# The linear attention's off-diagonal blocks over the array's column groups, in one PSUM tile for both parts of the sequence

## The chip, the cores and the metric

The kernel runs on one core of a Trainium2 chip. The metric is the device time of one execution in microseconds (us). TensorE (PE) multiplies matrices: it holds one operand, the weights, in its 128 by 128 array, streams the other past it and writes the result to PSUM. VectorE (DVE) and ScalarE (ACT) work elementwise and can read PSUM; GpSimd (POOL) and SyncE (SP) mostly issue transfers here.

## The reference

The reference is a trunk of two layers for one sequence of 256 positions and a width of 2048, in float32. Layer 0 has dilated sliding-window softmax attention in parallel with gated linear attention, layer 1 an S5 state-space part in parallel with HGRN2, which is gated linear attention again. Each layer has one input projection, a SiLU gate and one output projection, with RMSNorm before it. Cut to the part that the change is about:

```python
def chunked_gated_linear_attention(q, k, v, log_g):
    '''S_t = diag(g_t) S_{t-1} + k_t^T v_t ; o_t = q_t S_t, evaluated chunkwise.'''
    ...
        diff = bi[:, :, None] - bi[:, None, :]
        decay = jnp.exp(jnp.where(causal, diff, -jnp.inf))
        scores = jnp.einsum('bihk,bjhk,bijhk->bhij', qi, ki, decay)
        intra = jnp.einsum('bhij,bjhv->bihv', scores, vi)
```

So the score of query i and key j is the sum over the head's 128 channels of q times k times the product of the gates between j and i. Layer 0 does it for 4 heads, layer 1 for 8.

## The kernel before

**Projections.** `gemm_fm` (L174, matmul at L181) and `gemm_tm` (L193, matmul at L200) run through the weights in groups of 4 by 128 rows and 512 columns. `load_split` (L143) loads a group of 1 MB through SP's queue, rounds it to a high part `wh` on ScalarE (L168) and takes the rest `wl` on VectorE (L169); both are marked urgent and have three buffers. Three products per block (high by high, high by low, low by high) then go to a PSUM tile of the pool `pg`.

**Linear attention.** `gla` (L276) takes gates f, queries q and keys k as tiles of 128 channels by 4 heads by 256 positions. It is called once in layer 0 (L402) and twice in layer 1 (L675, four heads each). The scores go to the tile `AT` (named gA), which holds for each head three blocks of 128 keys by 128 queries: the first 128 positions with themselves (index 0), the first 128 as keys with the last 128 as queries (index 1), and the last 128 with themselves (index 2). The loop at L294 doubles a length h from 1 to 128. At level h the sequence falls into runs of 2h positions, and the queries in the second half of each run meet the keys in its first half. Between levels, VectorE multiplies the second halves of the queries (`Qp`, named gQ; L324) and the first halves of the keys (L325) by the gates over the next run (`Tc`), so that each level's product has its decay already in it.

- Levels 1 to 16 (`LV`): `small_blocks` (L281, matmul at L287) multiplies every 32 positions with themselves, and a masked copy (L296) picks what belongs to the level. Its four blocks of 32 write to partitions 0, 32, 64 and 96 of one PSUM tile in turn.
- Levels 32 and 64, the lines that change: for each of the two parts t of 128 positions there is a PSUM tile of its own. Each run of 2h positions, starting at j0, has one matmul per head (L308) of h keys by h queries over 128 channels; it writes to partitions j0 to j0 + h, the place that the block has in `AT`. A copy on VectorE per run (L311) brings all four heads' blocks to `AT`.
- Level 128: one matmul per head (L316) and a copy on ScalarE.

L339 then multiplies the scores with v.

**Order and buffers.** All of these tiles come from the pool `pm` (L65), four buffers of 128 partitions by 512 float32, which the softmax attention, the S5 part (L583, L622, L627) and its preparation (L1027) use too. L1027 and L622 multiply 128 rows by 64 weight columns and write to partitions 0 to 63 and 64 to 127 in turn. The order of the instructions on each engine is not that of the program text: a planner that simulates the run works it out when the kernel is built (L1126), with the urgent ones ahead, and it places the waits. On the chip each engine takes its instructions in that order.

Of the kernel before, what the change touches and what calls it, by code (L numbers as in the profile page):

```python
# [57 lines left out]
def trunk(ctx: ExitStack, tc: tile.TileContext, I, out):  # L58
    nc = tc.nc
    V, G, A, T = nc.vector, nc.gpsimd, nc.scalar, nc.tensor  # L60
# [26 lines left out]
    def col(o, n=1):  # L87
        return vec[:, o:o + n]

    def pm_tile(name="pm"):  # L90
        return pm.tile([128, 512], F32, name=name, tag="pm")

    def rsqrt(y, a, n, tag):
        it = small.tile([128, n], I32, name=tag + "i")
        ah = small.tile([128, n], F32, name=tag + "h")
        u = small.tile([128, n], F32, name=tag + "u")
        V.tensor_scalar(it, a.bitcast(I32), 1, None, op0=OP.logical_shift_right)
        V.tensor_scalar(y.bitcast(I32), it, -1.0, float(0x5F3759DF), op0=OP.mult, op1=OP.add)
        V.tensor_scalar(ah, a, -0.5, None, op0=OP.mult)
        for _ in range(3):  # L100
            V.tensor_tensor(u, y, y, op=OP.mult)
            V.tensor_tensor(u, u, ah, op=OP.mult)
            V.scalar_tensor_tensor(y, u, 1.5, y, op0=OP.add, op1=OP.mult)
# [70 lines left out]
    def gemm_fm(src, groups, ah, al, mid=None, order=None):  # L174
        ps = pg.tile([128, 4, S], F32, name="pg")
        last = groups * 4 - 1
        for i, kt, wh, wl in _iter(src, groups, mid, order):
            for n, (w, a) in enumerate(((wh, ah), (wh, al), (wl, ah))):
                for c in range(4):
                    cs = slice(c * 128, (c + 1) * 128)  # L180
                    state["mm"] = T.matmul(ps[:, c], w[:, cs], a[:, kt],  # L181
                                           start=(i == 0 and n == 0 and c % 2 == 0),
                                           stop=(i == last and n == 2), skip_group_check=True)
        return ps
# [8 lines left out]
    def gemm_tm(src, groups, ah, al, mid=None, order=None):  # L193
        ps = pg.tile([128, 2, 512], F32, name="pg")
        last = groups * 4 - 1
        for i, kt, wh, wl in _iter(src, groups, mid, order):
            for n, (w, a) in enumerate(((wh, ah), (wh, al), (wl, ah))):
                for t in range(2):
                    ts_ = slice(t * 128, (t + 1) * 128)
                    state["mm"] = T.matmul(ps[:, t], a[:, kt, ts_], w, start=(i == 0 and n == 0),  # L200
                                           stop=(i == last and n == 2), skip_group_check=True)
        return ps
# [5 lines left out]
    def bc(ap, n):  # L208
        return ap[:, None, :].to_broadcast([128, n, ap.shape[1]])

    def gla_tiles():
        return (mix.tile([128, 4, S], F32, name="gf"), mix.tile([128, 4, S], F32, name="gq"),
                mix.tile([128, 4, S], F32, name="gk"))
# [26 lines left out]
    f, q, k = gla_tiles()  # L240
# [30 lines left out]
    AT = const.tile([128, 4, 3, 128], F32, name="gA")  # L271
# [4 lines left out]
    def gla(f, q, k, v, dv, o0, rc=None):  # L276
        Qp = mix.tile([128, 4, S], F32, name="gQ")
        Dg = mix.tile([128, 2, 4, 32], F32, name="gD")
        V.tensor_mul(Qp, q, f)

        def small_blocks(Q):  # L281
            ps = pm_tile()[:, 0:256].rearrange("p (t h i) -> p t h i", t=2, h=4)
            for t in range(2):
                for hd in range(4):
                    for b in range(4):
                        r = slice(t * 128 + 32 * b, t * 128 + 32 * b + 32)
                        T.matmul(ps[32 * b:32 * b + 32, t, hd], k[:, hd, r], Q[:, hd, r], start=True, stop=True)  # L287
            return ps.rearrange("p t h i -> p (t h) i")

        Df = Dg.rearrange("p t h i -> p (t h) i")  # L290
        V.tensor_mul(Df, small_blocks(q), bc(cst[:, C_ID32:C_ID32 + 32], 8))
        Tc = f
        h = 1
        while True:  # L294
            if h in LV:
                V.copy_predicated(Df, bc(msk[:, LV.index(h)], 8), small_blocks(Qp))  # L296
                if h == LV[-1]:
                    for b in range(4):
                        r = slice(32 * b, 32 * b + 32)
                        for t in range(2):  # L300
                            A.activation(AT[r, :, 2 * t, r], Dg[r, t], AF.Copy)
            elif h < 128:
                for t in range(2):
                    ps = pm_tile().rearrange("p (h i) -> p h i", h=4)
                    for j0 in range(0, 128, 2 * h):
                        for hd in range(4):
                            b = t * 128 + j0
                            T.matmul(ps[j0:j0 + h, hd, j0 + h:j0 + 2 * h], k[:, hd, b:b + h],  # L308
                                     Qp[:, hd, b + h:b + 2 * h], start=True, stop=True)
                    for j0 in range(0, 128, 2 * h):  # L310
                        V.tensor_copy(AT[j0:j0 + h, :, 2 * t, j0 + h:j0 + 2 * h],  # L311
                                      ps[j0:j0 + h, :, j0 + h:j0 + 2 * h])
            else:
                ps = pm_tile()
                for hd in range(4):
                    T.matmul(ps[:, hd * 128:(hd + 1) * 128], k[:, hd, 0:128], Qp[:, hd, 128:256],  # L316
                             start=True, stop=True)
                A.activation(AT[:, :, 1], ps.rearrange("p (h i) -> p h i", h=4), AF.Copy)
                break
            nb = 4 * S // (2 * h)  # L320
            Qv = Qp.rearrange("p a s -> p (a s)").rearrange("p (n two h) -> p n two h", two=2, h=h)
            Kv = k.rearrange("p a s -> p (a s)").rearrange("p (n two h) -> p n two h", two=2, h=h)
            Tv = (Tc.rearrange("p a s -> p (a s)") if h == 1 else Tc).rearrange("p (n two) -> p n two", two=2)
            V.tensor_mul(Qv[:, :, 1], Qv[:, :, 1], Tv[:, :, 0:1].to_broadcast([128, nb, h]))  # L324
            V.tensor_mul(Kv[:, :, 0], Kv[:, :, 0], Tv[:, :, 1:2].to_broadcast([128, nb, h]))  # L325
            Tn = mix.tile([128, nb], F32, name=f"gT{h}")
            V.tensor_mul(Tn, Tv[:, :, 0], Tv[:, :, 1])
            Tc = Tn
            h *= 2
        o = [mix.tile([128, 4, dv], F32, name="go", tag=n) for n in ("gf", "gQ")]  # L330
        ssq = small.tile([128, 2, 4], F32, name="ssq")
        junk = mix.tile([128, 256], F32, name="junk", tag="gT1")
        hp = 512 // dv
        for t in range(2):
            for h0 in range(0, 4, hp):
                ps = pm_tile()
                for hd in range(h0, h0 + hp):
                    for j in range(t + 1):
                        T.matmul(ps[:, (hd - h0) * dv:(hd - h0 + 1) * dv], AT[:, hd, t + j],  # L339
                                 v[:, j, hd * dv:(hd + 1) * dv], start=(j == 0), stop=(j == t))  # L340
                A.activation(o[t][:, h0:h0 + hp], ps.rearrange("p (h d) -> p h d", d=dv), AF.Copy,
                             scale=1.0 if rc is None else rc[:, t:t + 1])
                for hd in range(h0, h0 + hp):
                    A.activation(junk[:, 0:dv], o[t][:, hd], AF.Square, accum_out=ssq[:, t, hd:hd + 1])
        ms = small.tile([128, 8], F32, name="hms")
        V.tensor_scalar(ms, ssq.rearrange("p a b -> p (a b)"), 1.0 / dv, EPS, op0=OP.mult, op1=OP.add)
        rs = small.tile([128, 8], F32, name="hrs")
        rsqrt(rs, ms, 8, "hr")
        for t in range(2):
            for hd in range(4):  # L350
                A.activation(og[:, t, o0 + hd * dv:o0 + hd * dv + dv], o[t][:, hd], AF.Copy,
                             scale=rs[:, t * 4 + hd:t * 4 + hd + 1])
# [23 lines left out]
    for h0 in range(0, 4, 2):  # L376
        ps = pm_tile().rearrange("p (n s) -> p n s", n=2)
        for n in range(2):
            T.matmul(ps[:, n], wgt[:, (h0 + n) * 128:(h0 + n + 1) * 128], glo, start=True, stop=True)
        for n in range(2):  # L380
            b = col(V_BG + h0 + n)
# [160 lines left out]
    for b in range(2):  # L542
        ps = gemm_fm(w1[b], 4, xh, xl)
# [119 lines left out]
    for half in range(2):  # L663
        f, q, k = gla_tiles()
# [24 lines left out]
    for b in range(2):  # L689
        ps = gemm_fm(I["wg"][b], 2, yh[:, 8:16], yl[:, 8:16])  # L690
# [54 lines left out]
    for b in range(3):  # L745
        res, h2 = residual(b)
        ps = gemm_tm(I["wo1"][b], 4, yh, yl, order=(2, 3, 0, 1))
# [4 lines left out]
    for half in range(2):  # L752
        ps = pg.tile([128, 2, 512], F32, name="pg")
# [385 lines left out]
```

## Time and profile before

| | |
|---|---|
| median of 3 runs | 888.54 us (887.33 to 891.26) |
| the profiled execution | 894.61 us, of which the span is 892.7 us |
| TensorE busy, granted clock | 874.1 us, 0.996 |
| VectorE, ScalarE busy | 636.0 us, 473.1 us |
| records at L308 | 144, the first at 131.7 us, the last at 710.9 us |
| moved from and to memory | 180.40 MB, a mean of 202 GB/s |

The span runs from the first instruction to the last. In the profile L308 is line 308, `pm<-gQ,gk` a group's output and inputs by the program's names, and PEld the loading of weights. Each float32 matmul of L287, L308, L622 and L1027 leaves two records, so that a count there is twice the number of matmuls. A record of TensorE lasts longer than its share of the stream, as matmuls overlap; what a group takes is read from the start of its first record to the start of the next group.

### The profile page before, as it was taken

The numbers are of one execution on the slowest core, as the hardware profiler recorded it, in microseconds if no ns is written. First come the engines' busy times: TensorE is split into PE (matmuls) and PEld (weight loads), VectorE is DVE, ScalarE is ACT, GpSimd is POOL, SyncE is SP. The second block draws the span as 40 slices with busy tenths as digits, with TensorE's granted clock in tenths as the row PEclk, the third lists the DMA queues.
The fourth block names the chain that finished last, engine by engine and source line by source line (L and its number), as shares of the span: only waits on it lengthen the run. The fifth ranks groups of instructions, "written<-read, shape, count | busy, mean of one in ns | idle before, by whom it ended". The sixth has DMA issues, their size and how long they took to land.

```text
span 892.7 us, 18688 instructions
## 1 busy us (share of the span) xinstructions
PE 874.1 (98%) x7728; PEld 804.5 (90%) x7728; DVE 636.0 (71%) x1197; ACT 473.1 (53%) x715; POOL 54.4 (6%) x106
## 2 busy tenths in 40 slices
PE   8999999999999999999999999999999999999995
PEld 8987899888998899999999999899867899988894
DVE  7987975888869868755575586877977655665562
ACT  7654546665655765644443345455545475444451
POOL 0001100111101101000000001100110000000000
PEclk9999999999999999999999999999999999999998
DMA  9827744777756655555575766754654455544432
GB/s 316 318 99 217 257 159 146 231 253 217 264 193 220 223 179 182 206 189 189 190 270 195 267 211 227 247 192 166 222 170 160 183 189 189 189 171 179 176 136 94
DMA packets 40388, 180.40 MB, mean 202 GB/s; under 512 B 12720, under 2 KB 14256, under 8 KB 22768
## 3 DMA queue, kind: packets, MB, share of 16 engines
q1 hardware_dynamic: 29440, 154.99, 49.5%
q0 software_dynamic: 7984, 22.69, 7.7%
q10 hardware_dynamic: 2880, 1.54, 0.6%
q8 instruction: 60, 0.98, 0.4%
q14 instruction: 24, 0.20, 0.1%
HBM read 166.48 MB, written 12.71 MB: 201 GB/s over the span
## 4 chain that ended last, share of the span: by engine, by line
PE 74%; DVE 8%; ACT 6%; DMA 5%; issue 5%; SPq 0%; POOL 0%; POOLq 0%; DVEq 0%; ACTq 0%
PE pg L181 48%; PE pg L200 17%; DVE wl L169 2%; PE pg L758 2%; DMA tabs<-pc 2%; ACT wh L168 1%; PE pm L287 1%; DMA E<-ed 1%; PE pm L339 1%; DMA s5y<-ys 1%; ACT bb L1021 1%; DMA raw<-in_w_dram 1%; ACT x L1039 1%; PE pm L308 1%; DVE PP L1005 1%
## 5 line engine op out<-in xcount | busy, mean ns | idle before, releaser
L168 ACT ACTIVATE wh<-raw 128x1024 fp32r<-128x1024 f32 (+2 forms) x276 | 287.6, 1046 | 325.0 <-PE pg L181 187.6
L169 DVE TENSOR_TENSOR wl<-raw,wh 128x1024 fp32r<-128x1024 f32 (+2 forms) x276 | 332.6, 1207 | 173.7 <-ACT wh L168 165.0
L181 PE MATMUL pg<-xh,wh 128*128 128x256 f32 x1024 | 162.8, 281 | 1.8 <-ACT wh L168 1.7
L181 PE MATMUL pg<-xl,wh 128*128 128x256 f32 x1024 | 163.8, 280 | 0.0
L181 PE MATMUL pg<-xh,wl 128*128 128x256 f32 x1024 | 163.4, 281 | 0.1
L181 PEld LDWEIGHTS pg<-xh,wh 128*128 128x128 f32 x1024 | 137.4, 188 | 3.7 <-ACT wh L168 3.1
L181 PEld LDWEIGHTS pg<-xl,wh 128*128 128x128 f32 x1024 | 138.0, 188 | 0.8 <-issue 0.3
L181 PEld LDWEIGHTS pg<-xh,wl 128*128 128x128 f32 x1024 | 137.9, 189 | 0.8 <-DVE wl L169 0.3
L200 PE MATMUL pg<-wh,xh 128*128 128x512 f32 x320 | 100.4, 395 | 1.8 <-ACT wh L168 1.8
L200 PE MATMUL pg<-wl,xh 128*128 128x512 f32 x320 | 101.0, 396 | 0.5 <-DVE wl L169 0.4
L200 PE MATMUL pg<-wh,xl 128*128 128x512 f32 x320 | 101.0, 395 | 0.0
L200 PEld LDWEIGHTS pg<-wh,xh 128*128 128x128 f32 x320 | 59.3, 188 | 14.8 <-ACT wh L168 2.2
L200 PEld LDWEIGHTS pg<-wl,xh 128*128 128x128 f32 x320 | 59.5, 188 | 14.1 <-DVE wl L169 1.3
L200 PEld LDWEIGHTS pg<-wh,xl 128*128 128x128 f32 x320 | 59.9, 188 | 12.8
L181 PE MATMUL pg<-yh,wh 128*128 128x256 f32 x320 | 50.8, 281 | 0.0
L181 PE MATMUL pg<-yl,wh 128*128 128x256 f32 x320 | 50.6, 281 | 0.0
L181 PE MATMUL pg<-yh,wl 128*128 128x256 f32 x320 | 50.6, 281 | 0.0
L181 PEld LDWEIGHTS pg<-yl,wh 128*128 128x128 f32 x320 | 43.4, 190 | 0.1
L181 PEld LDWEIGHTS pg<-yh,wh 128*128 128x128 f32 x320 | 43.2, 189 | 0.1
L181 PEld LDWEIGHTS pg<-yh,wl 128*128 128x128 f32 x320 | 43.1, 189 | 0.0
L967 POOL DMA_DIRECT2D tabs<-pc x44 | 23.8, 546 | 167.0 <-DVE x L977 43.7
L200 PE MATMUL pg<-wh,yh 128*128 128x512 f32 x96 | 30.1, 394 | 0.0
(350 smaller groups left out, 994.0 us busy)
## 6 DMA issues: line engine op xcount, KB each, us to landing
raw<-in_w_dram SPq DMA_DIRECT2D x100, 1024.0 KB, 5.0
raw<-in_wo_dram SPq DMA_DIRECT2D x28, 1024.0 KB, 4.8
tb<-tabs POOLq DMA_DIRECT2D x8, 768.0 KB, 6.4
tabs<-pc POOLq DMA_DIRECT2D x20, 256.0 KB, 5.7
raw<-in_wg_dram SPq DMA_DIRECT2D x4, 1024.0 KB, 4.8
raw<-in_wo1l_dram SPq DMA_DIRECT2D x4, 1024.0 KB, 4.8
raw<-in_w_dram SPq DMA_DIRECT2D x6, 512.0 KB, 7.4
tabs<-pc POOLq DMA_DIRECT2D x24, 128.0 KB, 4.9
```

Of the source, the lines that this page charges most:

```text
L168: state["wh"] = A.activation(w, r, AF.Copy)
L169: V.tensor_sub(l, r, w)
L181: state["mm"] = T.matmul(ps[:, c], w[:, cs], a[:, kt], start=(i == 0 and n == 0 and c % 2 == 0), stop=(i == last and n == 2), skip_group_c ...
L200: state["mm"] = T.matmul(ps[:, t], a[:, kt, ts_], w, start=(i == 0 and n == 0), stop=(i == last and n == 2), skip_group_check=True)
L287: T.matmul(ps[32 * b:32 * b + 32, t, hd], k[:, hd, r], Q[:, hd, r], start=True, stop=True)
L308: T.matmul(ps[j0:j0 + h, hd, j0 + h:j0 + 2 * h], k[:, hd, b:b + h], Qp[:, hd, b + h:b + 2 * h], start=True, stop=True)
L339: T.matmul(ps[:, (hd - h0) * dv:(hd - h0 + 1) * dv], AT[:, hd, t + j], v[:, j, hd * dv:(hd + 1) * dv], start=(j == 0), stop=(j == t))
L758: T.matmul(ps[:, t, 0:256], a_[:, kt, ts_], w_, start=(kt == 0 and n == 0), stop=(kt == KT - 1 and n == 2), skip_group_check=True)
L967: nc.gpsimd.dma_start(tabs[qt, dst, n], t[src].rearrange("p a b -> p (a b)"))
L1005: V.scalar_tensor_tensor(PP[half[1 - g], g].rearrange("p a b c -> p (a b c)"), x1[half[g]], -1.0, x2[half[g]], op0=OP.mult, op1=OP.subtract)
L1021: A.activation(bb[half[g ^ n], g], z[n][half[g]].unsqueeze(2).to_broadcast([64, 8, 4, 16]), AF.Copy)
L1039: A.activation(v8(x1)[:, r_], cst[:, C_ID64:C_ID64 + 64], AF.Copy, scale=vec[:, V_D + 8 * qt + r_:V_D + 8 * qt + r_ + 1])
```

## The change

At levels 32 and 64 both parts of the sequence now share one PSUM tile. Run n of the whole sequence (four at h = 32, two at h = 64) writes its four heads' blocks to partitions h n to h n + h, in the first 4h columns of the tile, and the inner loop goes over the runs, not over the heads. The copies bring each run's block from there to the same place in `AT` as before. The numbers of matmuls (16 and 8) and of copies (4 and 2) per call stay, and so do their sizes.

```diff
             elif h < 128:
-                for t in range(2):
-                    ps = pm_tile().rearrange("p (h i) -> p h i", h=4)
-                    for j0 in range(0, 128, 2 * h):
-                        for hd in range(4):
-                            b = t * 128 + j0
-                            T.matmul(ps[j0:j0 + h, hd, j0 + h:j0 + 2 * h], k[:, hd, b:b + h],
-                                     Qp[:, hd, b + h:b + 2 * h], start=True, stop=True)
-                    for j0 in range(0, 128, 2 * h):
-                        V.tensor_copy(AT[j0:j0 + h, :, 2 * t, j0 + h:j0 + 2 * h],
-                                      ps[j0:j0 + h, :, j0 + h:j0 + 2 * h])
+                ps = pm_tile()[:, 0:4 * h].rearrange("p (h i) -> p h i", h=4)
+                for hd in range(4):
+                    for n in range(128 // h):
+                        b = 2 * h * n
+                        T.matmul(ps[h * n:h * n + h, hd], k[:, hd, b:b + h], Qp[:, hd, b + h:b + 2 * h],
+                                 start=True, stop=True)
+                for n in range(128 // h):
+                    t, j0 = divmod(2 * h * n, 128)
+                    V.tensor_copy(AT[j0:j0 + h, :, 2 * t, j0 + h:j0 + 2 * h], ps[h * n:h * n + h])
             else:
```

## The prediction

> **What bounds the kernel now.** I read the page first, then who waited for whom, the timeline of TensorE around the bursts that the change rewrites, and the grouped lines of VectorE.
>
> ```profile
> span 892.7 us, 18688 instructions
> PE 874.1 (98%) x7728; PEld 804.5 (90%) x7728; DVE 636.0 (71%) x1197; ACT 473.1 (53%) x715; POOL 54.4 (6%) x106
> PEclk9999999999999999999999999999999999999998
> ```
>
> TensorE is busy for 98% of the span at full granted clock, VectorE for 71%. A busy row can hide waiting, so the waits of TensorE come next (columns: who waited for whom, total us, times, longest).
>
> ```profile
> PE pg L200 <- ACT wh L168: 1.8, 1, 1.8
> PE pg L181 <- ACT wh L168: 1.7, 3, 0.7
> PE pm L435 <- ACT pT L433: 1.2, 1, 1.2
> PE pm L287 <- DVE gk L325: 1.1, 1, 1.1
> ...
> PE pg L758 <- DVE h L721: 0.5, 1, 0.5
> PE pg L200 <- DVE wl L169: 0.4, 2, 0.2
> PE pm L431 <- DVE pr L428: 0.4, 1, 0.4
> ```
>
> These rows add up to 7.1 us in 892.7. So TensorE's own time sets the end, and time taken off its stream should reach the end unless one of these few waits swallows it. The linear attention stands inside that stream: its matmuls come as short bursts between the projections' matmuls.
>
> **The change part by part.** L308 issues, per call of gla, 16 matmuls at h = 32 and 8 at h = 64; the trace has two records for each (float32), so 32 and 16 records a burst. gla is called three times, which makes six bursts. The time that a burst takes from the stream is its start to the start of the next projection matmul:
>
> ```profile
> 131.73 0.90 PE L308 MATMUL pm<-gQ,gk 128*32 128x32 f32 x32
> 132.56 0.39 PE L181 MATMUL pg<-xl,wh 128*128 128x256 f32 x1
> ...
> 137.54 1.14 PE L308 MATMUL pm<-gQ,gk 128*64 128x64 f32 x16
> 138.62 0.62 PE L181 MATMUL pg<-xh,wh 128*128 128x256 f32 x3
> ```
>
> That is 0.83 us and 1.08 us. The other four bursts agree, the middle call's in the chain that ended last (start, us, what) and the last call's in the timeline:
>
> ```profile
> 601.88 0.83 PE pm L308 x32
> ...
> 607.12 1.07 PE pm L308 x16
> ```
>
> ```profile
> 702.79 0.90 PE L308 MATMUL pm<-gQ,gk 128*32 128x32 f32 x32
> 703.62 0.50 PE L200 MATMUL pg<-wh,xl 128*128 128x512 f32 x1
> ...
> 710.02 1.15 PE L308 MATMUL pm<-gQ,gk 128*64 128x64 f32 x16
> 711.10 0.50 PE L200 MATMUL pg<-wh,xh 128*128 128x512 f32 x1
> ```
>
> The number and shape of the matmuls stay; what changes is where each writes, and so which columns of the array hold its weights. Before, at h = 64 all eight write partitions 0 to 63; at h = 32 four in a row write 0 to 31, then four 64 to 95. Afterwards neighbours go to different places: 0, 32, 64, 96 in turn at h = 32, and 0, 64 in turn at h = 64. The trace has both patterns already. L622 alternates between partitions 0 and 64 with 64 weight columns and 64 moving ones, 16 records like h = 64; L1027 does the same 32 times; L287 goes round all four places with 32 by 32, 64 records or, in a fragment, 4.
>
> ```profile
> 534.21 0.69 PE L622 MATMUL pm<-X,tb 128*64 128x64 f32 x16
> 534.82 0.56 PE L627 MATMUL pm<-t,tb 64*64 64x63 f32 x12
> ...
> 335.27 1.15 PE L1027 MATMUL pm<-PP,bb 128*64 128x64 f32 x32
> 336.35 0.88 PE L504 MATMUL pm<-cst,gz 128*128 128x128 f32 x6
> ...
> 126.87 0.76 PE L287 MATMUL pm<-gQ,gk 128*32 128x32 f32 x64
> 127.56 0.61 PE L181 MATMUL pg<-xh,wl 128*128 128x256 f32 x3
> ...
> 103.54 0.26 PE L287 MATMUL pm<-gq,gk 128*32 128x32 f32 x4
> 103.73 0.73 PE L200 MATMUL pg<-wl,xh 128*128 128x512 f32 x2
> ```
>
> At h = 64 the new burst is L622's: 16 records in 0.61 us, where L308 takes 1.08: a gain of 0.47. At h = 32 it lies on L287's line: 64 records take 0.69 and 4 take 0.19, so one costs (0.69 - 0.19)/60 = 0.0083 us and the fixed part is 0.16; 32 records come to 0.16 + 32 x 0.0083 = 0.42, where L308 takes 0.83: a gain of 0.41. Together 0.88 us per call and **2.64 us** for three.
>
> A rule speaks against this. The Trainium skill, page "TensorE: Matmul & The Clock Gate", section "Part 3: Packing small matmuls — row/col tiling", says that a weight load overlaps running matmuls only when its row group differs; all these matmuls use all 128 rows, so by that rule the sum would be 0. The trace disagrees: at the same 128 rows and 64 columns L308 takes 1.08 us for 16 records, L1027 1.08 us for 32. Part 2 of that page, section "Back-to-back issue gap", gives small matmuls an issue floor of about 25 ns; by it 32 records would need an estimated 0.8 us and h = 32 would gain nothing. The trace disagrees there too: 64 records of L287 take 0.69 us.
>
> For the unknown size of the overlap I keep both ends: nothing gained, 0; and all fixed parts gone too, 2.64 + 6 x 0.16 = 3.6 us. I take 2.64, since L622 is the same shape in the same order.
>
> **VectorE.** The copies of L311 stay 18 in number and keep their shapes and destinations. Their source becomes contiguous and starts at partition h n. Rows of such copies, and the one that reads a whole contiguous PSUM row block:
>
> ```profile
> L169 DVE TENSOR_TENSOR wl<-raw,wh 128x1024 fp32r<-128x1024 f32 x270 | 329.5, 1222 | 172.1 <-ACT wh L168 163.5 <-ACT junk L344 3.6 <-PE pg L181 2.7
> ...
> L296 DVE COPY_PREDICATED gD<-msk,pm 128x256 f32<-128x256 int32 x15 | 6.7, 448 | 1.6 <-PE pm L287 1.3
> L311 DVE COPY gA<-pm 32x128 f32<-32x128 f32 x12 | 3.4, 283 | 0.8 <-PE pm L308 0.7
> L311 DVE COPY gA<-pm 64x256 f32<-64x256 f32 x6 | 2.4, 410 | 2.3 <-PE pm L308 2.3
> ```
>
> I count no change. The upper end is L296's 448 ns for every copy, 12 x 0.165 + 6 x 0.038 = 2.2 us; nothing reads faster here, but the strided read may cost something today, so the lower end is as far below nothing: 2.2 us off. VectorE's 172 us of idling before L169 cover either; if that cover were gone, 2.2 us would be the price.
>
> With one tile, the first copy waits for all the matmuls of its level, where before it waited for half. Behind it on VectorE stand the other copies, the next level's products (L324, L325) and the next L169. In the last call the first copies began like this:
>
> ```profile
> 703.42 1.18 DVE L311 COPY gA<-pm 32x128 f32<-32x128 f32 x4 [0.66 <-PE pm L308]
> ...
> 710.74 0.42 DVE L311 COPY gA<-pm 64x256 f32<-64x256 f32 x1 [1.50 <-PE pm L308]
> ```
>
> The copy at h = 64 comes 0.72 us after its burst's start (710.02), for half of the matmuls. L1027 less L622 gives 0.47/16 = 0.029 us a record in alternation, and so a fixed part of 0.61 - 16 x 0.029 = 0.14. All 16 are then through in the 0.47 us in which eight went before (half of 1.08 - 0.14): the same moment. At h = 32 the copy came at 0.63, half of the burst being through at (0.83 - 0.16)/2 = 0.34; all 32 records now need 32 x 0.0083 = 0.27, so it comes no later. **The added wait costs nothing**; if the overlap fails it costs half a burst, 0.4 to 0.5 us of VectorE, under the same cover.
>
> One of the four buffers of pm is taken per level where it was two. No row of TensorE's waits names a release of pm, so I count nothing. But the order of instructions on each engine is worked out at build by a planner that simulates durations (L1126), and six fewer takes of pm can move it. Nothing in the trace prices that; its bounds are rivals below.
>
> **The sum.** Profiled execution: 892.7 - 2.64 = 890.1 us of span (its own time is 894.61, so 892.0). The median of the runs is 888.54, 6.1 below that execution; off it the sum is **885.9 us**, 0.30% less. A difference of 0.5%, 4.4 us, is about what a measurement can tell from no change here, so I expect no change that shows: faster begins at 884.1, slower at 893.0.
>
> **Rivals.**
>
> *No overlap, or swallowed time.* If the new places don't overlap, the time stays 888.5; L622 and L287 speak against it. If only h = 64 gains, because a record can't follow faster than in today's h = 32 bursts (0.83/32 = 0.026 us), it is 888.54 - 3 x 0.47 = 887.1; L287's 0.0083 speaks against it. Or the first call's 0.88 us is swallowed by the next long wait:
>
> ```profile
> 214.04 0.70 PE L435 MATMUL pm<-pT,gv 128*128 128x256 f32 x2 [1.15 <-ACT pT L433]
> ...
> 205.17 6.32 DMA tabs<-pc
> ```
>
> Ahead of it in the chain that ended last stands a transfer whose length TensorE doesn't set. If it started no earlier, the result is 888.54 - 1.76 = 886.8; but that chain reaches back through rows of L169, which TensorE paces, so it should move along.
>
> *A wait in place of the gain: slower.* The planner may put the bursts too early for VectorE, as happened once:
>
> ```profile
> 116.17 0.68 DVE L325 TENSOR_TENSOR gk<-gk,gT 128x512 f32<-128x512 f32 x1
> ...
> 117.00 0.75 PE L287 MATMUL pm<-gQ,gk 128*32 128x32 f32 x64 [1.11 <-DVE gk L325]
> ```
>
> TensorE stood from the last projection matmul's end to 117.00 for a product that ended at 116.85. At the rewritten bursts the margin is small too:
>
> ```profile
> 604.78 0.69 DVE L325 TENSOR_TENSOR gk<-gk,gT 128x512 f32<-128x512 f32 x1
> ...
> 607.05 1.15 PE L308 MATMUL pm<-gQ,gk 128*64 128x64 f32 x16
> ```
>
> L325 ends at 605.47, 1.58 us ahead. It decides from there: a burst moved up by more than 1.58 us waits. If all six waited 1.2 us it would be 7.2 - 2.64 = 4.6 us more, **893.1 us**. For it: nothing fixes the order. Against it: the durations that the planner sees for the projections are unchanged, and only shorter or unchanged ones for the bursts.
>
> *A better order: faster.* If the new order sheds half of the 7.1 us of waits, the time is 888.54 - 2.64 - 3.55 = 882.3. For it: the waits are accidents of an order planned on simulated times; against it: none of them lies at the rewritten bursts.
>
> **How the numbers follow.** The forecast, order much as it is: 885.9, chance 0.58, of its own from 884.1 to 887.5. No overlap or swallowed: 886.8 to 888.5, chance 0.10. Better order, 880 to 884: 0.20. Waits and other misplanning, 888.5 to 895: 0.12, nearly all of it over 893.0 or close, of which I count 0.09 above. So faster 0.21, same 0.70, slower 0.09. The range from 881.5 to 890.5 takes in most of the better order and the end with nothing gained, and leaves out the two tails: some 0.08 below and 0.11 above. The end of 3.6 us lies in it (884.9).
>
> **What would show it.** L308's bursts should take 0.42 us (32 records) and 0.61 us (16) to the next projection matmul. If they still take 0.83 and 1.08, the overlap is wrong; if they shrink and the span doesn't, TensorE's waits should have grown, at L435 or L200, or at L308 itself behind L325. Copies at L311 should begin 0.5 to 0.7 us after their burst. What would make the prediction wrong is an order that differs far from these bursts: rows of waits over 1 us at places the diff doesn't touch.

## The result, and the profile after

| | median, us | range, us | runs |
|---|---|---|---|
| before | 888.26 | 886.62 to 891.83 | 16 |
| after | 893.71 | 889.33 to 899.91 | 16 |

The ratio is **1.0059**, with a 95% interval from 1.0038 to 1.0079: the changed kernel is slower, by 5.4 us between the medians, and lies above the predicted range. The profiled execution of after took 896.86 us, of which 895.0 us are its span. In the code after, every line behind the rewritten loop has a number one lower: L308 becomes L307, L508 becomes L507. In the experiments the lines behind the loop keep the numbers of before, except in e4, e5 and e7.

The page of after begins as the one of before did, with one digit that wasn't there: a dip of the granted clock in the middle of the span.

```profile
span 895.0 us, 18691 instructions
PE 873.4 (98%) x7728; PEld 801.9 (90%) x7728; DVE 635.3 (71%) x1197; ACT 472.5 (53%) x715; POOL 54.4 (6%) x106
PEclk9999999999999999899999999999999999999998
```

**The bursts gained what was forecast.** The timeline of TensorE in after (start, us, what), first the first call, then the middle and the last one:

```profile
131.49 0.46 PE L307 MATMUL pm<-gQ,gk 128*32 128x32 f32 x32
131.88 0.38 PE L181 MATMUL pg<-xl,wh 128*128 128x256 f32 x1
...
137.09 0.69 PE L307 MATMUL pm<-gQ,gk 128*64 128x64 f32 x16
137.70 0.39 PE L181 MATMUL pg<-xh,wh 128*128 128x256 f32 x1
...
604.89 0.46 PE L307 MATMUL pm<-gQ,gk 128*32 128x32 f32 x32
605.28 0.62 PE L181 MATMUL pg<-xl,wh 128*128 128x256 f32 x3
...
714.28 0.69 PE L307 MATMUL pm<-gQ,gk 128*64 128x64 f32 x16
714.89 0.73 PE L200 MATMUL pg<-wh,xl 128*128 128x512 f32 x2
```

From start to start that is 0.39 us at h = 32 (forecast 0.42) and 0.61 us at h = 64 (forecast 0.61). The six bursts together take 3.01 us where they took 5.71: 2.7 us less, against 2.64 forecast.

**More than that was lost elsewhere.** I numbered the projection matmuls of L181, L200 and L757 in the order in which TensorE issues them and compared their starts in the two profiles. No. 2100 starts at 358.12 us in after and at 361.79 us in before: after is 3.67 us ahead. No. 2250 starts at 382.54 against 379.52: it is 3.02 us behind. So 6.7 us went in one stretch, the start of layer 0's output projection, which the diff doesn't touch. (Most of the lead of 3.67 us is a delay of that one execution of before: in its second profile, e8, no. 2100 starts at 358.85 us, and after is 0.73 us ahead of it.) The view by windows of each profile (the window, its length, then busy time and instructions of TensorE, its weight loads, VectorE, ScalarE and GpSimd, the granted clock and the transfers' share), before and then after:

```profile
355.00:363.30 8.30, 8.30 (x76) 8.30 (x75) 5.82 (x9) 5.47 (x9) 0.56 (x2) 1.00 0.77 269
363.30:370.10 6.80, 6.80 (x59) 6.68 (x58) 6.80 (x11) 5.45 (x8) 0.00 (x0) 1.00 0.43 157
```

```profile
355.00:363.30 8.30, 6.12 (x52) 5.72 (x51) 5.95 (x9) 5.13 (x8) 0.00 (x0) 1.00 0.81 284
363.30:370.10 6.80, 5.64 (x25) 5.05 (x25) 6.57 (x9) 3.91 (x7) 0.00 (x0) 0.50 0.01 2
```

In these 15.1 us TensorE began 135 records before and 77 after. The 58 missing ones at 0.113 us each are 6.6 us. In the first window TensorE stands still for 2.2 us; in the second it waits again and has half its clock. The waits of after name what it stood for (who waited for whom, us in total, times, longest):

```profile
PE pg L181 <- DVE yl L507: 2.2, 2, 1.1
PE pg L181 <- ACT wh L168: 1.7, 3, 0.9
...
PE pg L181 <- ACT yh L506: 1.1, 1, 1.1
```

The first and the last row are new. Here `yh` and `yl` are the high and low part of the gated output of layer 0's linear attention, made on ScalarE and VectorE as the left operand of the output projection. The timeline of all engines in after shows the queue on each:

```profile
359.23 1.06 ACT L168 ACTIVATE wh<-raw 128x1024 fp32r<-128x1024 f32 x1 [1.66 <-PE pg L181]
359.68 1.29 DVE L358 TENSOR_TENSOR gz<-pg,r0b 128x512 f32<-128x512 f32 x2 [0.85 <-PE pg L181]
360.19 1.55 ACT L506 ACTIVATE yh<-pm,xv 128x256 fp32r<-128x256 f32 x4
...
360.70 0.72 PE L181 MATMUL pg<-yh,wh 128*128 128x256 f32 x4 [1.06 <-ACT yh L506]
360.89 1.22 DVE L169 TENSOR_TENSOR wl<-raw,wh 128x1024 fp32r<-128x1024 f32 x1
...
362.02 1.65 DVE L507 SCALAR_TENSOR_TENSOR yl<-pm,xv,yh 128x256 fp32r<-128x256 f32 x4
...
362.55 0.74 PE L181 MATMUL pg<-yl,wh 128*128 128x256 f32 x4 [1.13 <-DVE yl L507]
```

ScalarE idles 1.66 us for a weight buffer that TensorE still holds, rounds the weights, and only then makes `yh`. VectorE takes two gate products and a weight group ahead of `yl`. Each step starts when the one ahead of it in its queue is through, and TensorE, at the end of both queues, waits for both. In before the same instructions stood in another order:

```profile
359.69 1.57 ACT L507 ACTIVATE yh<-pm,xv 128x256 fp32r<-128x256 f32 x4 [1.17 <-DMA tabs<-pc]
...
360.20 1.66 DVE L508 SCALAR_TENSOR_TENSOR yl<-pm,xv,yh 128x256 fp32r<-128x256 f32 x4 [0.42 <-ACT yh L507]
...
363.15 0.62 PE L181 MATMUL pg<-yh,wh 128*128 128x256 f32 x4
...
363.61 0.62 PE L181 MATMUL pg<-yl,wh 128*128 128x256 f32 x4
```

There `yh` begins at 359.69 us and the product that reads it at 363.15, 3.5 us later: TensorE still had other projection work in front. Counted from the start of matmul no. 2100, `yh` begins 2.1 us ahead of it in before and 2.1 us behind it in after (360.19 against 358.12 us).

So two things changed together: the planner ordered TensorE, VectorE and ScalarE anew (SyncE's and GpSimd's instructions stand as before), and TensorE came earlier to a place whose cover, the time between the making of `yh` and its use, was 3.5 us. The theory to test: **the new order costs what was lost, the new bursts gain 2.7 us, and the conversions at 360 us are the main place.** The rivals: the new bursts or the shared tile themselves cost something later; or the loss is spread over the order and no single place explains it.

### The profile page after: what moved, and what is told of

The parts are those of the page before. It is cut to its first block, busy times and chain, and to the rows that moved or that the text cites. A ratio compares the mean times of both kernels' runs of the same rounds, so it can differ in the third digit from the quotient of the medians.

```text
span 895.0 us, 18691 instructions
## 1 busy us (share of the span) xinstructions
PE 873.4 (98%) x7728; PEld 801.9 (90%) x7728; DVE 635.3 (71%) x1197; ACT 472.5 (53%) x715; POOL 54.4 (6%) x106
## 4 chain that ended last, share of the span: by engine, by line
PE 88%; DVE 4%; issue 2%; DMA 2%; ACT 2%; SPq 0%; POOL 0%; DVEq 0%; POOLq 0%; ACTq 0%
PE pg L181 51%; PE pg L200 27%; PE pg L757 2%; PE pm L338 1%; PE pm L287 1%; DVE wl L169 1%; DMA yc<-s5y 1%; ACT wh L168 1%; DMA raw<-in_w_dram 1%; DMA s5y<-ys 1%; PE pm L414 1%; PE pm L582 1%; PE pm L626 1%; PE pm L1026 1%; PE pm L621 0%
## 5 line engine op out<-in xcount | busy, mean ns | idle before, releaser
L169 DVE TENSOR_TENSOR wl<-raw,wh 128x1024 fp32r<-128x1024 f32 (+2 forms) x276 | 332.2, 1207 | 176.7 <-ACT wh L168 172.5
L181 PE MATMUL pg<-xh,wh 128*128 128x256 f32 x1024 | 162.6, 280 | 1.7 <-ACT wh L168 1.7
L181 PE MATMUL pg<-xl,wh 128*128 128x256 f32 x1024 | 163.6, 279 | 0.0
L181 PE MATMUL pg<-xh,wl 128*128 128x256 f32 x1024 | 161.0, 279 | 0.1
L181 PEld LDWEIGHTS pg<-xh,wh 128*128 128x128 f32 x1024 | 137.1, 188 | 3.6 <-ACT wh L168 2.8
L181 PEld LDWEIGHTS pg<-xl,wh 128*128 128x128 f32 x1024 | 137.6, 188 | 0.8 <-issue 0.3
L181 PEld LDWEIGHTS pg<-xh,wl 128*128 128x128 f32 x1024 | 136.5, 188 | 0.8 <-DVE wl L169 0.3
L200 PE MATMUL pg<-wh,xh 128*128 128x512 f32 x320 | 101.5, 396 | 1.2 <-ACT wh L168 1.2
L200 PE MATMUL pg<-wl,xh 128*128 128x512 f32 x320 | 101.3, 397 | 0.8 <-DVE wl L169 0.6
L200 PE MATMUL pg<-wh,xl 128*128 128x512 f32 x320 | 100.5, 394 | 0.0
L200 PEld LDWEIGHTS pg<-wh,xh 128*128 128x128 f32 x320 | 59.2, 188 | 14.9 <-ACT wh L168 2.3
L200 PEld LDWEIGHTS pg<-wl,xh 128*128 128x128 f32 x320 | 59.0, 188 | 15.0 <-DVE wl L169 2.5
L200 PEld LDWEIGHTS pg<-wh,xl 128*128 128x128 f32 x320 | 60.1, 188 | 13.2
L181 PE MATMUL pg<-yl,wh 128*128 128x256 f32 x320 | 51.9, 285 | 2.2 <-DVE yl L507 2.2
L181 PE MATMUL pg<-yh,wh 128*128 128x256 f32 x320 | 51.8, 285 | 1.1 <-ACT yh L506 1.1
L181 PE MATMUL pg<-yh,wl 128*128 128x256 f32 x320 | 51.8, 284 | 0.0
L181 PEld LDWEIGHTS pg<-yl,wh 128*128 128x128 f32 x320 | 44.1, 192 | 2.7 <-DVE yl L507 2.7
L181 PEld LDWEIGHTS pg<-yh,wh 128*128 128x128 f32 x320 | 44.5, 193 | 1.7 <-ACT yh L506 1.6
L181 PEld LDWEIGHTS pg<-yh,wl 128*128 128x128 f32 x320 | 44.1, 192 | 0.0
L200 PE MATMUL pg<-wh,yh 128*128 128x512 f32 x96 | 30.1, 395 | 0.0
```

The lines of the kernel that those rows point to most:

```text
L169: V.tensor_sub(l, r, w)
L181: state["mm"] = T.matmul(ps[:, c], w[:, cs], a[:, kt], start=(i == 0 and n == 0 and c % 2 == 0), stop=(i == last and n == 2), skip_group_c ...
```

## The experiments

To part the order from the code, some kernels are held to a recorded order. Each engine's instructions get an edge from one to the next, with no wait in it, so that the planner has nothing left to choose:

```diff
         trunk(tc, I, out)
+        pin_order(tc)
```

```python
def pin_order(tc):
...
    for name, steps in plan.items():
...
            if prev is not None:
                tc.add_manual_dep(ins, prev.name, mybir.DependencyInfo(
                    mybir.DependencyClass.NoSync, mybir.DependencyReason.DATA), reason="order")
```

| | bursts | order | median, us | ratio to before, 95% interval |
|---|---|---|---|---|
| e1 | new | old | 885.53 | 0.9977 (0.9958 to 0.9996) |
| e2 | old | new | 898.35 | 1.0112 (1.0086 to 1.0137) |
| e3 | new | new, four groups moved | 888.27 | 1.0007 (0.9996 to 1.0019) |
| e4 | shared tile, no rotation | its own | 890.50 | 1.0043 (1.0025 to 1.0061) |
| e5 | new | new (the change again) | 896.45 | 1.0083 (1.0053 to 1.0113) |
| e6 | new | new, whole place nearly as before | 890.78 | 1.0026 (1.0004 to 1.0048) |
| e7 | rotation, a tile per part | its own | 889.00 | 1.0009 (0.9992 to 1.0025) |
| e9 | new | old, then new | 888.12 | 0.9999 (0.9974 to 1.0024) |
| e10 | new | new, then old | 891.70 | 1.0052 (1.0029 to 1.0075) |
| e11 | new | old (e1 again) | 885.41 | 0.9967 (0.9955 to 0.9979) |
| e12 | new | e10's, four groups moved | 887.34 | 0.9990 (0.9969 to 1.0010) |

### e1: the change in the order of before

The edit: the kernel after, with `pin_order` and the order of before.

> The change itself, with every engine's instructions held to the order that the kernel before had. Theory A (the order costs the time): the bursts keep their gain of 2.7 us, the waits at the first output projection are gone, and the time is 885 to 886.5 us, a ratio of 0.996 to 0.998 to the kernel before. Theory B (the new bursts or the shared tile cost the time by themselves): it stays near 893, a ratio of 1.004 to 1.008.

The ratio was 0.9977. The bursts take 0.39 and 0.61 us, and no wait for `yh` or `yl` is in the profile. The new bursts don't cost; in the old order they bring about what the sum said. This kernel is faster than both. Nor does an early TensorE bring the waits: here it starts no. 2100 at 357.94 us, as early as in after, and yet `yh` begins at 355.91 us and the product that reads it at 359.30, with 3.4 us of cover. In the old order the conversions come forward with the rest.

### e2: the bursts of before in the order of the change

The edit: the kernel before, with `pin_order` and the order of after.

> The kernel before, with every engine's instructions held to the order that the change brought. Theory A: slower by what the order costs, 892 to 897 us, a ratio of 1.004 to 1.010; the waits of TensorE for yh and yl at the first output projection are back. Theory B: as before, a ratio of 0.998 to 1.002.

1.0112, the slowest of all. Its waits:

```profile
PE pg L181 <- DVE yl L508: 2.7, 2, 1.6
...
PE pg L181 <- ACT yh L507: 1.4, 2, 1.1
```

Without a line of the change's arithmetic, the order alone brings a loss and the waits at 360 us, though TensorE starts no. 2100 at 359.29 us, 1.2 us later than in after. e1 and e2 exchange code and order: the new code in the old order has 0.9977, the old code in the new order 1.0112. The profile is of the fastest of its six executions, 892.76 us; the other five took 895.8 to 900.3 at a lower mean clock (0.989 to 0.994 against 0.997), so the profile shows where the order costs and not all that it costs.

### e3: one place mended

The edit, in the order of after: at layer 0's output projection, the conversions are taken ahead of the work they stood behind.

```diff
 ACT
+  yh L507 x4, first group
   wh L168
-  yh L507 x4, first group
+  yh L507 x4, second group
   yh L486
   gz L476
-  yh L507 x4, second group
 DVE
+  yl L508 x4, first group
   gz L359 x2
   wl L169
-  yl L508 x4, first group
+  yl L508 x4, second group
   yl L487
   gz L485
-  yl L508 x4, second group
```

> The change in its own order, but for four groups of four instructions: ScalarE's and VectorE's conversions of the gated heads to yh and yl are moved ahead of the instruction groups that stood before them. If that one place (some 360 us in) makes most of the loss, the waits for yh and yl go (3.3 us), no half-clock stretch follows them (3.4 us where it came), and the time falls to 886 to 889.5 us, a ratio of 0.998 to 1.001, with a smaller spread of the runs. If the loss lies in the order elsewhere, or in the bursts (theory B), it stays above 891.

1.0007 where the change has 1.0059 (and 1.0083 in e5). Sixteen moved instructions take back most of the loss against e1. Waits of 1.3 us for `yl` and 0.4 for `yh` are left, so the place isn't wholly mended.

### e4: a shared tile without the rotation, and e7: the rotation with a tile per part

These split the change itself. Each is planned anew. e4 shares the tile and issues the heads in the inner loop; e7 rotates and keeps two tiles.

```diff
-                for hd in range(4):
-                    for n in range(128 // h):
+                for n in range(128 // h):
+                    for hd in range(4):
```

> The change, but with the heads in the inner loop, so that four matmuls in a row go to the same columns; the planner orders it anew. Theory A: the bursts take about as long as before (0.7 to 0.83 us and 1.0 to 1.08 us), and the time is that of whichever order comes out, anywhere from 887 to 897; no link to the bursts. Theory B with the shared tile at fault: a ratio of 1.006 or more.

```diff
-                ps = pm_tile()[:, 0:4 * h].rearrange("p (h i) -> p h i", h=4)
+                pss = [pm_tile()[:, 0:4 * h].rearrange("p (h i) -> p h i", h=4) for _ in range(2)]
...
-                        T.matmul(ps[h * n:h * n + h, hd], k[:, hd, b:b + h], Qp[:, hd, b + h:b + 2 * h],
+                        T.matmul(pss[b // 128][h * n:h * n + h, hd], k[:, hd, b:b + h], Qp[:, hd, b + h:b + 2 * h],
```

> Matmuls and columns as in the change, but each part of the sequence keeps a PSUM tile of its own; the planner orders it anew. If sharing the tile is what the planner's order comes from, this returns to the order of before and gains: 885 to 887 us, a ratio of 0.996 to 0.999. If any small edit brings another order, it waits at the first output projection or elsewhere: 888 to 895 us, a ratio of 1.001 to 1.008. The bursts take 0.4 and 0.6 us in either case.

e4: its bursts take 0.83 us at h = 32, as before, and 0.90 at h = 64, 5.17 us in all, so four fifths of the gain belong to the rotation. Its ratio is 1.0043, and it has the waits of e2, 2.7 us for `yl` and 1.4 for `yh`. e7: its bursts take 0.39 and 0.61 us in two tiles, so the gain doesn't need the shared tile. But its planner put the conversions at 360 us where the change's did, and its profile has the same 2.2 and 1.1 us of waits. Its 1.0009 lies between the two ranges given for it and decides nothing by itself. Up to 610 us all its engines take the change's order, as those of e4 do; behind that its planner found another one, in which the projection matmuls no. 4000 to 5000 take 176.1 us, against 179.0 in e10 (the new order first, then the old). So a plan can lose at 360 us and win some of it back later. Since either half of the edit alone brings the bad place, the shared tile is not its cause by itself. What the two halves have in common is that all the copies of a level now follow all its matmuls in the program; whether that moved the plan wasn't tried.

### e5 and e8: after and before once more

> The changed kernel itself, once more, beside the other runs of this group. Theory A: TensorE waits for yh and yl at the first output projection as in its first profile (3.3 us in all), since the order is the same; whether the half-clock stretch follows may differ between executions, and so the spread stays at several us. Time 890 to 896 us, a ratio of 1.003 to 1.008. If the waits are gone in this profile, they were an accident of one execution.

> The kernel before, for a second profile of the same program. In its first profile a projection matmul took 118 ns in the output projection of layer 0 (360 to 465 us), where other profiles show 113. If the pace differs between executions of one program, this one may show 113 there, and a span shorter by some 4 us (888 in place of 892.7); if it belongs to the program, it shows 118 again. No wait for yh or yl of over 0.2 us in either case.

e5 came to 1.0083, so the first result was no chance. Its profile has the waits for `yl` and `yh` of e2, and a second place besides:

```profile
PE pg L200 <- ACT wh L168: 5.8, 2, 3.5
```

In the timeline of ScalarE in e5, the gelu of the S5 part waits twice for the return of its transfer, with the next weights queued behind it:

```profile
652.52 0.63 ACT L642 ACTIVATE gw<-yc 128x512 f32<-128x512 f32 x1 [7.74 <-DMA yc<-s5y]
653.06 1.04 ACT L168 ACTIVATE wh<-raw 128x1024 fp32r<-128x1024 f32 x1
...
678.90 0.63 ACT L642 ACTIVATE gw<-yc 128x512 f32<-128x512 f32 x1 [9.12 <-DMA yc<-s5y]
679.43 1.04 ACT L168 ACTIVATE wh<-raw 128x1024 fp32r<-128x1024 f32 x1
```

The same wait exists in the old order (1.4 us in e1, 0.9 in e11), so here the order is one cause among others. e8, a single execution of 887.82 us, served to compare paces; it is read in the last section.

### e6: the place mended in full

The edit: as e3, but the gate products stand behind the conversions too, with the next weights between them, nearly in the sequence of before. Two things still differ from before on both engines: one more weight group stands ahead of the first conversions, and the wide conversion (`yh` L486, `yl` L487) stands behind the second group of four and not behind the first.

> The change in its own order, but at the first output projection ScalarE and VectorE take the same instructions in the sequence in which the kernel before has them (conversions of the heads first, the next weights between). Theory A: no wait of over 0.5 us is left there, and the time falls below that of the mend of four groups (888.3) to 884.5 to 887.5 us, a ratio of 0.996 to 0.999. If the rest of the loss lies at 650 to 700 us, it stays at 1.000 to 1.001.

A miss: 1.0026, no better than e3, with intervals that overlap. Yet its profile shows the place nearly mended: 0.6 us for `yl` and 0.6 for `yh`, and from projection matmul no. 2000 to no. 2250 it takes 30.0 us, against 35.8 in after, 31.1 in e3 and 28.6 in e1 (after and e3 ran this part at the slower pace of the last section, which is worth 0.7 us here: before takes 29.1, e8 28.3). A loss like that of e5 stands at 650 us: a wait of 1.8 us for `wh` and half a clock behind it. So something was left beyond the first place, and the order was cut in two to find it.

### e9, e10, e11: the order in two halves

The edit: the change, held to one order up to the end of layer 0 and to the other from there on. e9 has the old one first, e10 the new one first, e11 the old one throughout.

> The change, held to the order of the kernel before up to the second half of layer 0 (the first gla call and the first output projection, with nothing moved there) and to the change's own order from the second gla call on. Theory A (two places cost: layer 0's output projection at 360 us, and the second layer's weight conversions on ScalarE, which stand behind a gelu that waits for the return of the y transfer at 640 to 690 us): the second place keeps the part that e3 and e6 did not get back, so 888 to 890 us, ratio 1.000 to 1.003, with TensorE waiting over 2 us for wh of L168 at L200 in many executions. Theory B (only the first place costs; what e3 and e6 left was still of that place): as e1, 885 to 886.5 us, ratio 0.997 to 0.9985.

> The other half: the change, in its own order up to the end of layer 0 and in the order of the kernel before from the second gla call on. Theory A: what the first place costs, 3 to 5 us over e1, 889 to 891.5 us, ratio 1.001 to 1.004. Theory B: all of the loss, 893 to 895 us, ratio 1.005 to 1.008. In either the waits for yh and yl at 360 us are in its profile.

> e1 a second time, beside the two halves: 885 to 887 us, ratio 0.996 to 0.999. If it is above 1.000, the gain of the bursts in the old order is not larger than what changes from one call to the next, and e1's number was luck.

Over e11 (0.9967), the early part of the new order costs 0.0085, or 7.6 us, and the late part 0.0032, or 2.8 us. e9 is what theory A gave; e10 is above its bound (1.004), though its interval reaches below it, and just within what theory B gave, so the early place is probably dearer than A had it. The late part's cost is less sure: the intervals of e9 and e11 overlap, and in e9's profile 3.2 of the 3.9 us that it loses on e11 come from a pace that changes between executions of the same order (last section). What of the 2.8 us is order and what is pace stays open. e11 repeats e1: the gain of the bursts in the old order is 0.2 to 0.3%, or 2.0 to 2.9 us.

### e12: the early half with e3's repair

The edit: e10 with the sixteen moves of e3.

> e10 with the one repair of e3: the change's own order in the early part, the old order in the late one, and at layer 0's output projection the four groups of conversions (yh on ScalarE, yl on VectorE) taken ahead. If these conversions are what the early part of the new order costs, the 0.85% between e10 and e11 are gone but for what e3 left of the waits there (1.7 us in its profile): ratio 0.997 to 1.000, 885.5 to 888.5 us. If other moved instructions of the early part cost as well, it stays near e10: 1.003 to 1.005, 890 us or more.

0.9990. Of the 0.0085 between e10 and e11 the sixteen moves bring back 0.0062. In the waits of e10 and of e12:

```profile
PE pg L181 <- DVE yl L508: 2.7, 2, 1.6
...
PE pg L181 <- ACT yh L507: 1.4, 2, 1.1
```

```profile
PE pg L181 <- DVE yl L508: 1.3, 1, 1.3
...
PE pg L181 <- ACT yh L507: 0.5, 1, 0.5
```

4.1 us of waits became 1.8, and from matmul no. 2000 to no. 2250 e10 takes 33.6 us, e12 30.7 and e11 28.3. That stretch holds 5.2 of the 6.7 us by which e10's span is longer than e11's. The place is shown to be the main cost of the early part: taking sixteen conversions ahead, and nothing else, moves the time.

## Why the prediction was wrong, step by step

- **The bursts: right.** Forecast 0.42 and 0.61 us, 2.64 us in all; measured 0.39 and 0.61 us, 2.7 us in all. Both rules of the Trainium skill that were weighed against this (page "TensorE: Matmul & The Clock Gate", sections "Part 3: Packing small matmuls — row/col tiling" and "Back-to-back issue gap") fail here: the bursts got shorter with every matmul on all 128 rows, and 32 records pass in 0.39 us, 12 ns each.
- **VectorE's copies and the added wait: right.** The copies of L311 take 285 and 418 ns in after, where they took 283 and 410, and the first one at h = 32 in the last call starts 0.53 us behind its burst. At h = 64 it starts 1.5 us behind in the first and last call of after, because the new order puts a weight group (L169) ahead of it; in the old order (e1) it is 0.73 us, as forecast. TensorE's waits show nothing for either.
- **The swallowed 0.88 us at L435: didn't happen.** That wait belonged to one execution: the second profile of before, e8, doesn't have it either. The stretch with the first call's bursts, projection matmuls no. 750 to 1000, takes 42.73 us in before and e8 and 41.83 in after, 0.90 less, and at no. 2100 after is still 0.73 us ahead of e8.
- **"Six fewer takes of pm can move it. Nothing in the trace prices that": the step that failed.** The sum then went on with the order "much as it is", at a chance of 0.58. The order didn't stay: on TensorE and VectorE it changed from the first call's h = 64 burst on, on ScalarE from 186 us on. That cost 7 to 10 us, about three times what the bursts gain (new bursts: 1.006 and 1.008 in the new order, 0.998 and 0.997 in the old; old bursts in the new order: 1.011). The prediction's own sign of being wrong, waits over 1 us at places the diff doesn't touch, is what came. The trace of before couldn't tell that the planner would turn the conversions and the weights around, but it shows how little room there was: `yh` had 3.5 us of cover at 359.69 us, and a weight group put ahead of it takes 1.06 us on ScalarE, one put ahead of `yl` 1.2 us on VectorE. What the step lacked was a list of the places where TensorE's next operand is made on another engine shortly before it is read. Why these lines move the plan stays open.
- **The rival on the slower side: the kind was right, the place and the price were not.** It let TensorE wait at the bursts behind L325, for 4.6 us, at a chance of 0.12. The waits came at L181 behind L506 and L507, 220 us later. The time it gave, 893.1 us, is close to the 893.7 measured, but by another mechanism.
- **The range.** Its upper end, 890.5, came from leaving out that rival. With the order open, 897 would have belonged inside.

## What to carry to other kernels

Where a planner works out the order, an edit of a few instructions is also a new order for all of them, and the two have to be measured apart: hold the new code to the old order, and the old code to the new one. Look in the trace for operands that other engines finish only a few microseconds before TensorE reads them, and then in the new order for work that now stands ahead of their making; here most of such a loss came back by moving the conversions ahead of work that wasn't due. A TensorE that comes earlier is not the danger by itself: in e1 it came as early, and the conversions came forward with it. Here the change in its old order (e1, e11) is faster than both kernels, by 0.2 to 0.3% against before.

## What the runs showed of the hardware

**Half a clock followed waits of a few microseconds.** In after the granted clock fell to one half for 6.83 us, from 363.3 us on, though no wait there was over 1.2 us. e7 has the same at the same place; e5 and e6 have it for 3.41 us at 650 us, behind a single wait of 3.5 us in e5 and of 1.8 us in e6. The windows of e5:

```profile
645.00:655.60 10.60, 7.01 (x30) 5.12 (x29) 6.60 (x10) 3.05 (x4) 0.73 (x1) 1.00 0.37 125
655.60:659.00 3.40, 3.40 (x9) 2.62 (x9) 3.34 (x6) 2.79 (x4) 0.00 (x0) 0.50 0.00 0
659.00:670.00 11.00, 11.00 (x222) 8.84 (x221) 7.00 (x13) 4.25 (x6) 2.11 (x4) 1.00 0.64 216
```

The other ten profiles, e2, e4 and e10 among them with the waits at 360 us, have no such stretch inside the span, and only its end is at half clock. All four stretches are 3.413 us or twice that, and each begins and ends a whole number of 3.413 us after the clock first became full (105 and 107 of them in after and e7, 189 and 190 in e5, 188 and 189 in e6). Cut into such windows, the fourteen traces part cleanly by the time in which no matmul record runs on TensorE: each full-clock window with 1.82 us or more of it was followed by half a clock (e6 1.82, after 1.90, e5 2.04, e7 2.13), and none with 1.69 us or less was (before 1.69, e10 1.66, e2 1.64). So what counts here is the idle share of one window, about half of it, and the same waits can fall into one window or be split between two. The Trainium skill, page "TensorE: Matmul & The Clock Gate", section "Part 1: The HAM clock gate (the \"warmup\" mystery)", has a free-running window of 3413 ns, and the lengths agree; its rule that the clock falls after an idle window of about 3.4 us isn't what these runs show, since a window with about half of it idle sufficed. From matmul no. 2000 to no. 2250, e7 takes 35.2 us and e10, with the same bursts and order there at full clock, 33.6, so the half clock was worth some 1.6 us. Of the 16 runs of after, the five with a mean clock of 0.996 have a median of 890.46 us, the nine below 0.995 one of 895.2: the spread of the changed kernel goes partly with it.

**One stretch of matmuls has two paces.** TensorE runs the same output projection without a pause from 380 to 460 us in all profiles. The windows of that stretch, TensorE alone, in after and then in e5, the same kernel:

```profile
380.00:460.00 80.00, 80.00 (x681) 1.00 0.53 189
```

```profile
380.00:460.00 80.00, 80.00 (x708) 1.00 0.57 202
```

681 records are 117.5 ns each and 708 are 113.0, both at full granted clock. Before shows both as well: 682 in its first profile and 708 in e8. Four of the fourteen profiles have the slower pace (before, after, e3, e9), each for the whole of this projection. It costs about 3 us in this stretch alone, as much as the whole gain of the change, and it is why two profiles can't be compared by their spans here: the two of before differ by 6.7 us, of which 4.0 lie between matmul no. 2100 and no. 3000. What sets it stays open.
